# Decoder trunk on one core: another order for the opening loads, x converted chunk by chunk, 12 warm-up matmuls

## The chip, the cores and the metric

The kernel runs on one core of a Trainium2 chip. The metric is the device time of one execution in microseconds (us). The core's engines work side by side, each through its own list of instructions, and wait for each other by semaphores: TensorE (PE, matmuls), VectorE (DVE), ScalarE (ACT), GpSimd (POOL) and SyncE (SP, which here only issues DMA loads and stores). ACT and POOL can issue DMAs too.

## The reference

One layer of a decoder for 256 tokens of width 2048, in fp32. Cut to what matters here:

```python
h = rms_norm(x, ln_mix_pre)           # x * rsqrt(mean(x*x) + 1e-6) * gain
proj = h @ w_in                       # 2048 -> 6144: q, k, v of two head groups
o_sb = stick_breaking_attention(...)  # 8 heads
o_dl = dilated_mixture(...)           # 8 heads
o = rms_norm(concat(o_sb, o_dl), ln_head)
x = x + rms_norm(o @ w_out, ln_mix_post)
g, u = split(rms_norm(x, ln_ffn_pre) @ w_gate_up)
x = x + rms_norm((silu(g) * u) @ w_down, ln_ffn_post)
x = x + sigmoid(rms_norm(x, ln_pli) @ w_pli_gate) * (p @ w_pli_proj)
```

All weights are read once from HBM; that and the matmuls are most of the work. The change lies in the very first part, where h is formed and the first product h @ w_in starts.

## The kernel before

**Numbers as sums of two.** Every fp32 operand of a matmul is split into a rounded part and the remainder, `hi` and `lo`, and a product is three matmuls: hi·hi, hi·lo, lo·hi. For weights the split is line 107 (ACT, cast to `whi`) and line 108 (DVE, `wlo = wraw - whi`). For x it is done with the norm's gain at once: line 294 (ACT) makes `hT_hi = xT * g`, and line 295 (DVE) `hT_lo = xT * g - hT_hi`. The gain `g` is a column of `gT`, a tile of 128 x 64 fp32 with the scales of four norms, which is loaded once at line 197. The norm's other factor, one number a token, is applied after the product, where the banks are read out.

**The first projections.** x comes already transposed (`xT`), so that its 16 chunks of 128 features are the stationary sides of the matmuls. `gemm` walks over the 16 chunks in four groups of four (`KG`); a group's weights are three tiles, `wraw`, `whi`, `wlo`, of which the pool holds three sets (`bufs=3`). So the raw load of group 3 must wait until group 0's raw tile has been split, and so on. Each chunk takes six matmuls of 128 x 512 (two blocks of 128 tokens, three products), line 157. The first `gemm` is the projection to k of the stick-breaking heads; for it, `before=load_x` loads xT two chunks at a time (256 KB, into the memory of `y_sb`) just before the weights of these chunks are loaded (line 147). The second `gemm` (q) has `before=load_norm`: it loads x in its natural layout into the same `y_sb` (line 307), from which ACT computes the squares of the norm (line 222).

**What sets the order.** The code is written in the order of the work, but a planner sets each engine's list. Instructions inside `tc.high_priority(offset=WEIGHT_AHEAD)` rank as if they stood 200 places earlier in the code. Loads of xT and of weights, and their splits, are in such blocks; the load of gT is not. On each engine the planned list is then worked through strictly in order. A DMA that must wait, for a free buffer or for an earlier DMA that used the same semaphore, holds up all later ones of the engine that issues it.

**Warm-ups.** Before the real work PE runs ten matmuls on a zeroed tile (line 202) that feed nothing.

Of the kernel before, what the change touches and what calls it, by code (L numbers as in the profile page):

```python
# [27 lines left out]
WEIGHT_AHEAD = 200  # L28
# [6 lines left out]
def kernel(  # L35
# [38 lines left out]
    nc = tc.nc  # L74
    x, p, w_in, w_out = x[0], p[0, 0], w_in[0], w_out[0]
    w_gate_up, w_down, w_pli_gate, w_pli_proj = w_gate_up[0], w_down[0], w_pli_gate[0], w_pli_proj[0]
    out = out[0]
# [21 lines left out]
    gT = const.tile([P, 64], F32, name="gT")  # L99
# [17 lines left out]
    def tick(n=1):  # L117

        for _ in range(n):
            clock[0] += 1  # L120
            if pending and pending[0][1]():
                pending.popleft()[0]()
# [8 lines left out]
    class Chunk:  # L131
# [29 lines left out]
        def step(self, g, parts=None):  # L161

            c0, c1 = g * KG, min((g + 1) * KG, self.nk)
            halves = [(c, min(c + 2, c1)) for c in range(c0, c1, 2)]
            if parts is None:
                self.load(c0, c1)
            for a, b in halves:
                if parts is not None:
                    n = parts(a // 2)
                    for c in range(a, b, 2 // n):  # L170
                        self.load(c, c + 2 // n)
                for t in range(T):
                    self.mm(t, a, b)
                tick()
# [19 lines left out]
                evac(t, c.pm[t])  # L194


    nc.scalar.dma_start(out=gT, in_=gains)
    nc.scalar.preload_act_table_set("natural_log_exp_and_others")
    nc.vector.memset(junk, 0.0)
    warm = ps_m.tile()  # L200
    for _ in range(10):
        nc.tensor.matmul(warm, lhsT=junk[:, 0:P], rhs=junk, start=True, stop=True)
    make_identity(nc, ident)
    G_PRE, G_HEAD, G_FFN, G_PLI = 0, 16, 32, 48
# [14 lines left out]
    def token_rs(column, t):  # L219
        ss = sum_squares()  # L220
        for c in range(4):
            nc.scalar.activation(
                out=junk, in_=column(t, c), func=AF.Square,
                scale=1.0 / math.sqrt(D), accum_out=ss[:, c:c + 1])
        s1 = small.tile([P, 1], F32, name="s1")
        nc.vector.tensor_reduce(s1, ss, axis=mybir.AxisListType.X, op=ALU.add)
        return rsqrt(s1, 1)
# [41 lines left out]
    with tc.tile_pool(name="mixed", bufs=1) as mixed:  # L269
# [14 lines left out]
        xT_sb = y_sb.rearrange("q t (k m) -> q (t k) m", m=T * P)  # L284

        def load_x(g):

            with tc.high_priority(offset=WEIGHT_AHEAD):
                ks = slice(g * 2, (g + 1) * 2)
                nc.sync.dma_start(out=xT_sb[:, ks], in_=xT[:, ks])  # L290
                for kk in range(ks.start, ks.stop):
                    g_col = gT[:, G_PRE + kk:G_PRE + kk + 1]
                    h_hi = hT_hi[:, kk].rearrange("q t m -> q (t m)")
                    nc.scalar.activation(out=h_hi, in_=xT_sb[:, kk], func=AF.Copy, scale=g_col)
                    nc.vector.scalar_tensor_tensor(
                        out=hT_lo[:, kk].rearrange("q t m -> q (t m)"), in0=xT_sb[:, kk], scalar=g_col,
                        in1=h_hi.bitcast(F32), op0=ALU.mult, op1=ALU.subtract)
            return 2 if g < 2 else 1

        late = []  # L300

        def load_norm(g):

            if 1 <= g <= 4:
                sl = slice((g - 1) * NB, g * NB)
                with tc.high_priority(offset=WEIGHT_AHEAD):
                    nc.sync.dma_start(out=y_sb[:, :, sl], in_=x_v[:, :, sl])
            if g == 4:
                for t in range(T):
                    r = token_rs(lambda t, c: y_sb[:, t, c * NB:(c + 1) * NB], t)  # L310
                    rq = small.tile([P, 1], F32, name="rsq")
                    nc.vector.tensor_scalar(rq, r, 1.0 / math.sqrt(HD), None, ALU.mult)
                    rs.append(r)
                    rsq.append(rq)
                for evac, t, pm in late:
                    evac(t, pm)
            return 1


        zmask = mix.tile([P, 3, P], BF16, name="zmask")  # L320
# [1 line left out]
        for j in (0, 2):  # L322
            nc.gpsimd.affine_select(
                out=zmask[:, j, :], in_=zmask[:, j, :], pattern=[[1, P]], base=-1, channel_multiplier=-1,
# [7 lines left out]
            out=tri[:, 0:P], in_=tri[:, 0:P], pattern=[[-1, P]], base=-1, channel_multiplier=1,  # L332
# [47 lines left out]
        def parts(box, h, ts):  # L380
            x = box[0]
            if len(ts) == 2:
                return [x[:, i, h].rearrange("q t m -> q (t m)") for i in range(2)]
            return [x[:, i, h, ts[0]] for i in range(2)]
# [394 lines left out]
    def gate_out(k, np):  # L779
        s = [None, None]  # L780

        def out(t, n, x):
            with chain():
                if n == 0:
                    s[t] = temp()
                    silu(x, s[t], t)
                else:
                    gated(x, s[t], t)
                    hidden(k, np, t, s[t])
        return out  # L790
# [36 lines left out]
    parts = ((0, 4), (4, 8), (8, 11))  # L827
    for part, (j0, j1) in enumerate(parts):
        for j in range(j0, j1):
            out = gate_out(j - j0, 2 * (j1 - j0))  # L830
# [143 lines left out]
```

## Time and profile before

| | us |
|---|---|
| median of 3 runs | 1244.36 (1244.33 to 1245.23) |
| the profiled execution | 1244.12 |
| its span on the core | 1242.4 |
| gT's load issued (ACT) | 0.80 |
| first conversion of x starts (ACT) | 4.74 |
| first real matmul starts (PE) | 6.72 |

The span runs from the first instruction to the last one; 1.72 us of the execution's time lie around it. In rows of the timeline the first number is the start and the second the length, both in us, then engine, line, operation, written tile and read tiles; in square brackets stands how long the engine was idle before and what ended that. "SPq" and "ACTq" are DMA issues by these engines. In grouped rows the number behind the bar is the busy time, then the mean in ns.

### The profile page before, as it was taken

Reading aid. Unit: us, or ns where it says so; the run is one execution under the profiler, and the core shown is the slowest. Engines: PE = TensorE matmul, PEld = TensorE weight load, DVE = VectorE, ACT = ScalarE, POOL = GpSimd, SP = SyncE. Lnnn points to the kernel's source line nnn. Section 1 sums busy time; section 2 is a strip of 40 time slices with the busy share of each in tenths; the row PEclk is TensorE's granted clock in tenths of the full one; section 3 lists DMA queues with packets and bytes.
Section 4 is the critical chain, followed back from the end, with each engine's and each line's share of the span. In section 5 each row is a group of like instructions: output and inputs, shape, how many; then the busy total and the mean of one; then the engine's idle time right before and its main releaser. Section 6 shows DMA issues by size and latency. Waiting matters only on the chain.

```text
span 1242.4 us, 14323 instructions
## 1 busy us (share of the span) xinstructions
PE 1231.7 (99%) x5503; PEld 992.7 (80%) x5503; DVE 941.9 (76%) x975; ACT 652.3 (53%) x738; POOL 31.1 (3%) x57
## 2 busy tenths in 40 slices
PE   9999999999999999999999999999999999999997
PEld 6887888888888888888888888888777888887886
DVE  6575564545554868988888798889878888888887
ACT  6654554454443746555544555555453555655553
POOL 0001000000100200000000000000000000001000
PEclk9999999999999999999999999999999999999999
DMA  9744744455655845556555555655555565657761
GB/s 343 266 148 169 254 149 161 165 169 170 245 195 178 282 150 181 192 204 214 178 190 198 198 177 200 236 168 197 180 180 192 203 212 173 246 175 241 241 202 69
DMA packets 123172, 245.10 MB, mean 197 GB/s; under 512 B 6960, under 2 KB 7264, under 8 KB 122720
## 3 DMA queue, kind: packets, MB, share of 16 engines
q1 hardware_dynamic: 120320, 233.07, 55.2%
q0 software_dynamic: 2528, 11.02, 2.4%
q8 instruction: 43, 0.70, 0.2%
q14 instruction: 25, 0.20, 0.1%
q10 hardware_dynamic: 256, 0.10, 0.0%
HBM read 238.91 MB, written 6.83 MB: 198 GB/s over the span
## 4 chain that ended last, share of the span: by engine, by line
PE 93%; DVE 3%; ACT 1%; issue 1%; DMA 1%; POOL 0%; DVEq 0%; SPq 0%; ACTq 0%; POOLq 0%
PE bank L675 62%; PE bank L157 27%; DVE wlo L108 1%; ACT whi L107 1%; PE bank L686 1%; PE bank L378 1%; PE bank L233 1%; PE bank L348 1%; DMA wraw<-in_w_pli_gate_dram 0%; DMA gT<-in_gains_dram 0%; DVE temp L898 0%; PE bank L391 0%; PE bank L390 0%; PE bank L389 0%; PE bank L416 0%
## 5 line engine op out<-in xcount | busy, mean ns | idle before, releaser
L108 DVE TENSOR_TENSOR wlo<-wraw,whi 128x2048 fp32r<-128x2048 f32 (+3 forms) x229 | 465.2, 2040 | 198.3 <-ACT whi L107 197.7
L107 ACT CAST whi<-wraw 128x2048 fp32r<-128x2048 f32 (+3 forms) x229 | 390.5, 1709 | 371.0 <-PE bank L675 207.8
L675 PE MATMUL bank<-whi,hT_hi 128*128 128x512 f32 x667 | 262.5, 397 | 0.2 <-ACT whi L107 0.2
L675 PE MATMUL bank<-wlo,hT_hi 128*128 128x512 f32 x667 | 261.9, 395 | 0.5 <-DVE wlo L108 0.4
L675 PE MATMUL bank<-whi,hT_lo 128*128 128x512 f32 x667 | 261.6, 395 | 0.0
L157 PE MATMUL bank<-whi,hT_hi 128*128 128x512 f32 x384 | 157.2, 410 | 1.0 <-ACT whi L107 1.0
L157 PE MATMUL bank<-whi,hT_lo 128*128 128x512 f32 x384 | 152.3, 397 | 0.0
L157 PE MATMUL bank<-wlo,hT_hi 128*128 128x512 f32 x384 | 152.2, 396 | 0.0
L675 PEld LDWEIGHTS bank<-wlo,hT_hi 128*128 128x128 f32 x667 | 125.2, 188 | 31.7 <-DVE wlo L108 1.5
L675 PEld LDWEIGHTS bank<-whi,hT_hi 128*128 128x128 f32 x667 | 125.1, 188 | 30.6 <-ACT whi L107 0.9
L675 PEld LDWEIGHTS bank<-whi,hT_lo 128*128 128x128 f32 x667 | 125.2, 188 | 29.9
L649 DVE TENSOR_TENSOR wlo<-wsum,whi 128x2048 fp32r<-128x2048 f32 x47 | 107.6, 2288 | 12.9 <-ACT whi L648 12.8
L675 PE MATMUL bank<-wlo,fT_hi 128*128 128x512 f32 x282 | 111.2, 396 | 0.5 <-DVE wlo L108 0.5
L675 PE MATMUL bank<-whi,fT_hi 128*128 128x512 f32 x282 | 110.9, 397 | 0.2 <-ACT whi L107 0.2
L675 PE MATMUL bank<-whi,fT_lo 128*128 128x512 f32 x282 | 110.9, 396 | 0.0
L157 PEld LDWEIGHTS bank<-whi,hT_lo 128*128 128x128 f32 x384 | 72.5, 189 | 17.7
L157 PEld LDWEIGHTS bank<-whi,hT_hi 128*128 128x128 f32 x384 | 72.6, 189 | 16.8 <-ACT whi L107 1.9
L157 PEld LDWEIGHTS bank<-wlo,hT_hi 128*128 128x128 f32 x384 | 72.8, 189 | 14.5 <-DVE wlo L108 0.3
L641 DVE TENSOR_TENSOR wsum<-wraw 128x1024 f32<-128x1024 f32 x47 | 57.4, 1221 | 11.3 <-DMA wraw<-in_w_down_dram 5.9
L647 ACT CAST whi<-wsum 128x1024 fp32r<-128x1024 f32 x47 | 49.5, 1052 | 29.1 <-PE bank L675 27.8
L675 PEld LDWEIGHTS bank<-wlo,fT_hi 128*128 128x128 f32 x282 | 53.0, 188 | 14.1 <-DVE wlo L108 1.5
L675 PEld LDWEIGHTS bank<-whi,fT_hi 128*128 128x128 f32 x282 | 52.9, 188 | 13.4 <-ACT whi L107 0.9
(174 smaller groups left out, 1421.0 us busy)
## 6 DMA issues: line engine op xcount, KB each, us to landing
wraw<-in_w_gate_up_dram SPq DMA_DIRECT2D x176, 512.0 KB, 4.8
wraw<-in_w_down_dram SPq DMA_DIRECT2D x88, 512.0 KB, 5.2
wraw<-in_w_in_dram SPq DMA_DIRECT2D x40, 1024.0 KB, 5.2
wraw<-in_w_out_dram SPq DMA_DIRECT2D x16, 1024.0 KB, 5.0
wraw<-in_w_pli_gate_dram SPq DMA_DIRECT2D x32, 512.0 KB, 5.2
wraw<-in_w_in_dram SPq DMA_DIRECT2D x14, 512.0 KB, 8.3
y_sb<-in_xT_dram SPq DMA_DIRECT2D x8, 256.0 KB, 7.2
y_sb<-in_x_dram SPq DMA_DIRECT2D x4, 512.0 KB, 9.4
```

The costliest lines, as they stand in the source:

```text
L107: nc.scalar.copy(hi, raw)
L108: nc.vector.tensor_tensor(lo, raw, hi.bitcast(F32), ALU.subtract)
L157: nc.tensor.matmul(self.pm[t], lhsT=a[:, c, t, :], rhs=b[:, c % KG, :], start=c == 0 and a is a_hi and b is hi, stop=c == self.nk - 1 and ...
L233: nc.tensor.transpose(out=pt[:, k * P:(k + 1) * P], in_=x_sb[c][:, t, k * P:(k + 1) * P], identity=ident)
L348: nc.tensor.transpose(out=pt[:, h * P:(h + 1) * P], in_=nat[:, h * P:(h + 1) * P], identity=ident)
L378: nc.tensor.matmul(out, lhsT=a[u], rhs=b[w], start=i == 0, stop=i == 2)
L641: nc.vector.tensor_tensor(s[:, 0:2], raw[:, 0:1].to_broadcast([P, 2, NB]), raw[:, 1:4:2], ALU.add)
L647: nc.scalar.copy(shi[:, 0:2], s[:, 0:2])
L649: nc.vector.tensor_tensor(slo, s, shi.bitcast(F32), ALU.subtract)
L675: nc.tensor.matmul(pm, lhsT=a[u], rhs=w[v], start=first and x == 0 and y == 0, stop=last and x == len(terms) - 1 and y == 2)
L686: nc.tensor.transpose(out=pt[:, c * P:(c + 1) * P], in_=f[:, c * P:(c + 1) * P], identity=ident)
```

## The change

Three edits in the opening. The load of gT moves from ACT's instruction stream to SP's. The first piece of xT (chunks 0 and 1) is issued by ACT, the other seven by SP as before. The conversion of x leaves `load_x` for a function `convert_x`, which `step` calls for as many chunks as the next weight load covers: one at a time in the first two pairs of chunks, two at a time later. And there are 12 warm-up matmuls, not 10.

```diff
@@ Chunk.step
             for a, b in halves:
                 if parts is not None:
-                    n = parts(a // 2)
+                    n, convert = parts(a // 2)
                     for c in range(a, b, 2 // n):
+                        convert(c, c + 2 // n)
                         self.load(c, c + 2 // n)
@@ start of the program
-    nc.scalar.dma_start(out=gT, in_=gains)
+    nc.sync.dma_start(out=gT, in_=gains)
     nc.scalar.preload_act_table_set("natural_log_exp_and_others")
     nc.vector.memset(junk, 0.0)
     warm = ps_m.tile()
-    for _ in range(10):
+    for _ in range(12):
         nc.tensor.matmul(warm, lhsT=junk[:, 0:P], rhs=junk, start=True, stop=True)
@@ load_x
             with tc.high_priority(offset=WEIGHT_AHEAD):
                 ks = slice(g * 2, (g + 1) * 2)
-                nc.sync.dma_start(out=xT_sb[:, ks], in_=xT[:, ks])
-                for kk in range(ks.start, ks.stop):
+                (nc.sync if g else nc.scalar).dma_start(out=xT_sb[:, ks], in_=xT[:, ks])
+            return 2 if g < 2 else 1, convert_x
+
+        def convert_x(c0, c1):
+            with tc.high_priority(offset=WEIGHT_AHEAD):
+                for kk in range(c0, c1):
                     g_col = gT[:, G_PRE + kk:G_PRE + kk + 1]
                     h_hi = hT_hi[:, kk].rearrange("q t m -> q (t m)")
                     nc.scalar.activation(out=h_hi, in_=xT_sb[:, kk], func=AF.Copy, scale=g_col)
                     nc.vector.scalar_tensor_tensor(
                         out=hT_lo[:, kk].rearrange("q t m -> q (t m)"), in0=xT_sb[:, kk], scalar=g_col,
                         in1=h_hi.bitcast(F32), op0=ALU.mult, op1=ALU.subtract)
-            return 2 if g < 2 else 1
@@ load_norm
-            return 1
+            return 1, lambda c0, c1: None
```

The planned lists of three engines change in the opening. First SP's loads, from its first on (`y_sb<-in_xT_dram` is a piece of xT, `wraw` weights, a trailing x4 means four such rows). Before:

```order
L290 DMA y_sb<-in_xT_dram 128x512
L147 DMA wraw<-in_w_in_dram 128x512 x4
L290 DMA y_sb<-in_xT_dram 128x512 x2
L147 DMA wraw<-in_w_in_dram 128x2x512
L290 DMA y_sb<-in_xT_dram 128x512
L147 DMA wraw<-in_w_in_dram 128x2x512
```

In the change, the same list from the eleventh to the twenty-second load, with what each waits for (DMAHW is an earlier DMA's semaphore, DVE_49 a buffer that DVE has to free):

```order
L147 DMA wraw<-in_w_in_dram 128x2x512 [waits DMAHW3_49]
L291 DMA y_sb<-in_xT_dram 128x512 [waits DMAHW4_49]
L147 DMA wraw<-in_w_in_dram 128x2x512 [waits DMAHW5_49]
L291 DMA y_sb<-in_xT_dram 128x512 [waits DMAHW6_49]
L147 DMA wraw<-in_w_in_dram 128x2x512 [waits DMAHW7_49,DVE_49]
L291 DMA y_sb<-in_xT_dram 128x512 [waits DMAHW0_49]
L147 DMA wraw<-in_w_in_dram 128x2x512 [waits DMAHW1_49]
L147 DMA wraw<-in_w_in_dram 128x2x512 [waits DMAHW2_49,DVE_49]
L147 DMA wraw<-in_w_in_dram 128x2x512 [waits DMAHW3_49]
L147 DMA wraw<-in_w_in_dram 128x2x512 [waits DMAHW5_49,DMAHW4_49,DVE_49]
L147 DMA wraw<-in_w_in_dram 128x2x512
L198 DMA gT<-in_gains_dram 128x64 [waits DMAHW6_49]
```

The load of gT (line 198 of the new code) stands behind seven pieces of xT and fourteen weight loads, three of which wait for DVE; before it was ACT's first instruction. Behind it on SP come the four loads of x for the norm, the load of pT and the weights of the third group of the second projection. Second, ACT's list at the start of the program. Before:

```order
L197 DMA gT<-in_gains_dram 128x64
L198 ACT_TABLE_LOAD
L294 ACTIVATE hT_hi<-y_sb,gT 128x256 x2
L107 CAST whi<-wraw 128x512 x4
L294 ACTIVATE hT_hi<-y_sb,gT 128x256 x4
L107 CAST whi<-wraw 128x1024
L294 ACTIVATE hT_hi<-y_sb,gT 128x256 x2
```

In the change:

```order
L291 DMA y_sb<-in_xT_dram 128x512
L199 ACT_TABLE_LOAD
L107 CAST whi<-wraw 128x512 x4
L107 CAST whi<-wraw 128x1024 x4
L299 ACTIVATE hT_hi<-y_sb,gT 128x256 x16
L107 CAST whi<-wraw 128x1024 x2
L223 ACTIVATE junk,ss<-y_sb 128x512 x4
L107 CAST whi<-wraw 128x1024 x2
```

All sixteen conversions of x now stand in one block behind the casts of the first three groups of weights; the squares of the norm (line 223) and the casts follow. Third, DVE's list has moved the same way: before, its first work on x and on weights was

```order
L295 SCALAR_TENSOR_TENSOR hT_lo<-y_sb,gT,hT_hi 128x256 x2
L108 TENSOR_TENSOR wlo<-wraw,whi 128x512 x4
L295 SCALAR_TENSOR_TENSOR hT_lo<-y_sb,gT,hT_hi 128x256 x2
L334 CAST ntri<-tmp 128x128
L295 SCALAR_TENSOR_TENSOR hT_lo<-y_sb,gT,hT_hi 128x256 x2
```

and in the change it is

```order
L108 TENSOR_TENSOR wlo<-wraw,whi 128x512 x4
L338 CAST ntri<-tmp 128x128
L108 TENSOR_TENSOR wlo<-wraw,whi 128x1024 x4
L300 SCALAR_TENSOR_TENSOR hT_lo<-y_sb,gT,hT_hi 128x256 x16
L108 TENSOR_TENSOR wlo<-wraw,whi 128x1024 x2
```

DVE's splits of the first three groups stand ahead of all sixteen of x, and those that free the raw buffers for SP don't depend on gT. PE's list has the two more warm-ups and some swaps among the first matmuls, and is otherwise the same.

## The prediction

> **What bounds the kernel now.** I read the page first, for the share of each engine and the chain of waits.
>
> ```profile
> span 1242.4 us, 14323 instructions
> PE 1231.7 (99%) x5503; PEld 992.7 (80%) x5503; DVE 941.9 (76%) x975; ACT 652.3 (53%) x738; POOL 31.1 (3%) x57
> PE 93%; DVE 3%; ACT 1%; issue 1%; DMA 1%; POOL 0%; DVEq 0%; SPq 0%; ACTq 0%; POOLq 0%
> ```
>
> TensorE (PE) is busy in 99% of the span and carries 93% of the chain that ends last. Next I looked at what PE ever waits for, and at the stretch after its first real matmul.
>
> ```profile
> PE bank L202 <- DVE junk L199: 1.3, 1, 1.3
> PE bank L157 <- ACT whi L107: 1.0, 1, 1.0
> PE bank L675 <- DVE wlo L108: 0.9, 2, 0.5
> ...
> 6.72:1242.40 1235.68, 1227.30 (x5493) 991.37 (x5493) 939.53 (x965) 649.03 (x733) 29.54 (x47) 1.00 0.58 197
> ```
>
> The two longest waits of PE lie in the opening. After 6.72 us it is idle for 1235.68 - 1227.30 = 8.4 us, and part of that is the tail behind the last matmul. So a later first matmul moves the end by nearly the same amount: at most 8.4 us could be taken up. The one question is when the first L157 matmul starts. The timeline of the opening answers it for the kernel before:
>
> ```profile
> 0.80 0.41 ACTq L197 DMA_DIRECT2D gT<-in_gains_dram  x1
> 0.81 0.38 SPq L290 DMA_DIRECT2D y_sb<-in_xT_dram  x1
> 1.24 1.84 SPq L147 DMA_DIRECT2D wraw<-in_w_in_dram  x4
> 1.26 4.45 PE L202 MATMUL bank<-junk 128*128 128x512 bf16 x10 [1.26 <-DVE junk L199]
> 3.13 0.91 SPq L290 DMA_DIRECT2D y_sb<-in_xT_dram  x2
> 4.74 0.91 ACT L294 ACTIVATE hT_hi<-y_sb,gT 128x256 fp32r<-128x256 f32 x2 [2.20 <-DMA gT<-in_gains_dram]
> 5.28 0.88 DVE L295 SCALAR_TENSOR_TENSOR hT_lo<-y_sb,gT,hT_hi 128x256 fp32r<-128x256 f32 x2 [3.41 <-ACT hT_hi L294]
> 5.55 1.64 ACT L107 CAST whi<-wraw 128x512 fp32r<-128x512 f32 x3
> 6.72 1.22 PE L157 MATMUL bank<-whi,hT_hi 128*128 128x512 f32 x2 [1.02 <-ACT whi L107]
> ```
>
> ScalarE (ACT) waits for gT, the norm scales. They are asked for at 0.80 and usable at 4.74; conversion of x and of the weights follows, and PE starts at 6.72.
>
> **The change, part by part.** *The place of the gT load.* The line is now issued by sync (SP), but the planned order has it behind twenty-one others: seven of the eight pieces of xT (the first is on ScalarE's queue) and fourteen weight loads. Everything that makes hT waits for gT, and every real matmul reads hT. So I need gT's landing.
>
> Bytes ahead of it: xT, 8 pieces of 256 KB, is 2.10 MB; the weights are six groups of 1 MB, four of the first projection and two of the second (4 x 256 KB and 10 x 512 KB), 6.29 MB; together 8.39 MB. The sizes and their times to land stand in the DMA view of 0 to 60 us:
>
> ```profile
> wraw<-in_w_in_dram SPq DMA_DIRECT2D x14, 512.0 KB, 8.3
> y_sb<-in_xT_dram SPq DMA_DIRECT2D x8, 256.0 KB, 7.2
> wraw<-in_w_in_dram SPq DMA_DIRECT2D x4, 256.0 KB, 4.2
> gT<-in_gains_dram ACTq DMA_DIRECT2D x1, 32.0 KB, 3.9
> ```
>
> A 512 KB load takes 8.3 us here though the queue moves that much in 1.4 us at the rates below: loads of this queue wait behind those issued earlier. How fast they drain is in the windows (last two columns: DMA share and GB/s):
>
> ```profile
> 0.00:10.00 10.00, 7.72 (x18) 3.79 (x19) 5.00 (x16) 5.52 (x10) 1.53 (x10) 1.00 0.78 246
> 10.00:14.00 4.00, 4.00 (x19) 3.21 (x18) 3.25 (x8) 3.53 (x7) 0.00 (x0) 1.00 1.05 400
> 14.00:20.00 6.00, 6.00 (x28) 4.79 (x27) 5.79 (x8) 5.31 (x9) 0.00 (x0) 1.00 1.05 387
> 20.00:26.00 6.00, 6.00 (x27) 4.81 (x26) 4.60 (x7) 4.78 (x8) 0.00 (x0) 1.00 1.05 387
> ```
>
> The DMA share is full from 10 us on, so the rate cannot rise with another order. Moved by 10, 14, 20 and 26 us: 2.46, 4.06, 6.38 and 8.70 MB. The gap between "moved" and "usable" comes from three casts that waited for their weights:
>
> ```profile
> 12.88 1.05 ACT L107 CAST whi<-wraw 128x1024 fp32r<-128x1024 f32 x1 [0.19 <-DMA wraw<-in_w_in_dram]
> ...
> 14.90 1.05 ACT L107 CAST whi<-wraw 128x1024 fp32r<-128x1024 f32 x1 [0.16 <-DMA wraw<-in_w_in_dram]
> ...
> 16.93 1.05 ACT L107 CAST whi<-wraw 128x1024 fp32r<-128x1024 f32 x1 [0.16 <-DMA wraw<-in_w_in_dram]
> ```
>
> By the order of issue, 3.15, 3.93 and 4.72 MB had been asked for up to these loads; they are moved at 11.7, 13.7 and 15.7 us, and the casts start 1.2 us later each time.
>
> When does SP issue gT? The two weight loads just ahead need the third raw buffer back, which VectorE (DVE) frees when it has split the last half of group 2. In the new order that load too stands behind 4.72 MB, so it is usable at about 16.9, then cast and split:
>
> ```profile
> L108 DVE TENSOR_TENSOR wlo<-wraw,whi 128x1024 fp32r<-128x1024 f32 x14 | 17.2, 1225 | 7.8 <-ACT whi L107 7.6
> L107 ACT CAST whi<-wraw 128x1024 fp32r<-128x1024 f32 x14 | 14.7, 1047 | 4.6 <-DMA wraw<-in_w_in_dram 4.6
> L294 ACT ACTIVATE hT_hi<-y_sb,gT 128x256 fp32r<-128x256 f32 x16 | 7.0, 498 | 2.6 <-DMA gT<-in_gains_dram 2.2 <-DMA y_sb<-in_xT_dram 0.4
> L295 DVE SCALAR_TENSOR_TENSOR hT_lo<-y_sb,gT,hT_hi 128x256 fp32r<-128x256 f32 x16 | 6.9, 479 | 3.7 <-ACT hT_hi L294 3.7
> ...
> 19.27 0.88 SPq L147 DMA_DIRECT2D wraw<-in_w_in_dram  x2
> ```
>
> 16.9 + 1.05 + 1.23 with small steps between is 19.3; two issues of 0.44 us each bring gT's own issue to 20.2. By then 6.46 MB have moved, so 1.93 MB are still ahead: 5.0 us, to 25.2. gT's 32 KB take 0.1 us, and 1.2 us of landing make **26.5**. ScalarE then makes the first piece of hT in the 0.54 us that lie between its 4.74 and DVE's 5.28 above, and PE starts at **27.05**, 20.3 us later than 6.72. All weights of three groups are split by then, and three more groups lie raw in the buffers.
>
> *Behind the start.* ACT and DVE convert one chunk of x in about 0.45 us each (498 and 479 ns, starts overlapping), and PE uses six matmuls on it, 1.4 us at the spacing of the row below: no second wait there. Behind gT on SP stand the four loads of x for the norm, pT, and the weights of group 6. The x loads need parts of y_sb that DVE frees 4.4 to 7.1 us after the start; the last lands by about +11; the squares, at 0.75 us each, let pT go at +10 and group 6 at +11.5, landing near +15. PE reaches group 6 after 144 matmuls, 33.6 us. The cover is 18 us, less about 10 for the casts that wait for their buffers and for nat, so 8 us: I cost it at nothing.
>
> *Chunk by chunk conversion, x's first load on ScalarE's queue, two more warm-ups.* With gT at 26.5 none of these is on the path: the first x has landed 20 us earlier, and twelve warm-ups end at 1.26 + 12 x 0.43 = 6.4 us, inside PE's wait. Their cover is that wait; without it two warm-ups would cost 0.85 us. pT's earlier split only uses DVE's time beside PE.
>
> *The slow first matmuls.* The matmul row of the opening against the steady pace:
>
> ```profile
> 8.17 0.63 PE L157 MATMUL bank<-whi,hT_lo 128*128 128x512 f32 x1
> 8.60 0.63 PE L157 MATMUL bank<-whi,hT_hi 128*128 128x512 f32 x1
> ...
> 9.88 0.43 PE L157 MATMUL bank<-wlo,hT_hi 128*128 128x512 f32 x1
> 10.15 0.39 PE L157 MATMUL bank<-whi,hT_lo 128*128 128x512 f32 x1
> ...
> 107.80 11.20 PE bank L157 x48
> ```
>
> Matmuls start every 0.43 us up to 9.88 and every 0.233 us (11.20 / 48) later, while the clock column stays at 1.00. Eight real matmuls are slow, at 8 x 0.195 = 1.6 us. Now PE rests for some 20 us, which no row before shows. Bounds: no slow matmul at all, -1.6; or as many as in the whole opening, 10 + 8, +1.9. The nearest row is the start from rest at 1.26, where all ten warm-ups (4.45 us) stayed slow, so at least two more than eight; I take +0.5.
>
> The Trainium skill, "TensorE: Matmul & The Clock Gate", Part 1, says that an idle window of some 3.4 us halves PE's clock and that one busy window of the same length, running freely, restores it. By that rule the restart costs an estimated 1.5 to 3.1 us against the 1.6 of now, so the end would be 20.3 to 21.8 us later; the spacing at 1.26 and 9.88 agrees with it, and a long gap is not in this trace.
>
> *Sum.* The profiled execution took 1244.12 us, 1.72 more than its span and 0.24 less than the median. 1244.1 + 20.3 + 0.5 = **1264.9 us**.
>
> **Rivals.** *The small load overtakes.* If gT's packets don't wait for the 1.93 MB, it lands the 3.9 us of its row after its issue: 20.2 + 3.9 = 24.1, PE starts at 24.65, and the time is 1262.5. For it: 32 KB is small. Against: the 8.3 us of the 512 KB loads. The Trainium skill's "DMA: Bandwidth & Descriptors", Queues, rings and completion order, has each engine consume one queue's descriptors in ring order, against this rival; the row on 512 KB agrees.
>
> *The loads behind gT come too late.* SP sits in the wait for DVE with the queue empty, and ScalarE's squares hold back pT and with it group 6. If the 8 us of cover is missed by 4, the time is 1269. For it: ACT's order now has four squares ahead of the casts of the second projection. Against: the slack above, and the raw weights already loaded.
>
> *gT does come first, as the few words say.* Then it is usable at 4.7 as now, only one chunk is converted ahead of its weights, and the twelve warm-ups set the start: 6.6 instead of 6.72, with no gap in which the clock falls back, at best 1.6 us less. That gives 1242.5 to 1244: not slower. It decides if SP sends gT ahead of the weights. Against: SP's rows before (one piece of xT, four of weights, two of xT) are its planned list in order.
>
> *It is absorbed.* PE's idle 8.4 us would leave +12: 1256. Against: those gaps wait for DVE and for weights at places that shift with the start.
>
> **How the numbers follow.** The forecast has 0.80, overtaking 0.06, late loads 0.06, gT first 0.04, absorbed 0.02, and 0.02 is for what I don't see (half of it faster). The forecast's own bounds: the early drain could be as fast as the later one (400 GB/s from 4 us on: 1.0 us earlier), landing up to 1 us later, slow matmuls -1.6 to +1.9; one us off each way in issue. Taken together 1262.3 to 1267.3; with overtaking and a part of the late loads the range is 1261.6 to 1267.8. About 0.2%, 2.5 us, is what a measurement can tell from no change. Even "gT first" ends within 0.2% of the 1244.4 shown, so it makes up no change: 0.04; faster 0.01 and slower 0.95, where "absorbed", "late loads" and "overtaking" all fall.
>
> **What would show it.** In the profile after: ACT's first hT_hi (L299) near 26.5 with gT named as what ended some 8.5 us of idle; SP's gT (L198) issued near 20; PE's first L157 near 27 with an idle time of about 20 us; gaps below 1 us afterwards; DMA nearly still from 27 to 31 us. It is wrong if gT is issued among SP's first loads, if PE starts before 23 us, or if PE has a second wait of over 2 us before 70 us.

## The result, and the profile after

| | before | after |
|---|---|---|
| median | 1244.67 us (1244.33 to 1245.23, 4 runs) | 1264.43 us (1263.87 to 1264.55, 4 runs) |
| the profiled execution | 1244.12 us | 1264.35 us |
| its span | 1242.4 us | 1262.6 us |

The ratio of after to before is 1.0161, with a 95% interval of 1.0146 to 1.0176: the change makes the kernel slower by 1.6%, near 20 us.

The page of the kernel after, its span, its engines and the shares of the chain of waits:

```profile
span 1262.6 us, 14327 instructions
PE 1232.9 (98%) x5505; PEld 993.8 (79%) x5505; DVE 942.0 (75%) x975; ACT 652.2 (52%) x738; POOL 31.0 (2%) x57
PE 92%; DVE 3%; DMA 2%; ACT 1%; issue 1%; SPq 0%; POOL 0%; DVEq 0%; ACTq 0%; POOLq 0%
```

PE's busy time has grown by 1.2 us and the span by 20.2. So PE does nothing for some 19 us more than before. What it waits for stands in its waits (total, times, longest, in us), the first rows:

```profile
PE bank L157 <- ACT hT_hi L299: 19.8, 1, 19.8
PE bank L679 <- DVE wlo L108: 1.3, 3, 0.5
PE bank L203 <- DVE junk L200: 1.3, 1, 1.3
```

One wait of 19.8 us, for the first piece of hT; the next is 1.3 us in three parts. The timeline of the opening shows how that wait is made:

```profile
0.80 0.42 ACTq L291 DMA_DIRECT2D y_sb<-in_xT_dram  x1
0.81 1.33 SPq L147 DMA_DIRECT2D wraw<-in_w_in_dram  x3
1.26 5.30 PE L203 MATMUL bank<-junk 128*128 128x512 bf16 x12 [1.26 <-DVE junk L200]
...
12.10 7.30 SPq L147 DMA_DIRECT2D wraw<-in_w_in_dram  x5
...
16.18 1.04 ACT L107 CAST whi<-wraw 128x1024 fp32r<-128x1024 f32 x1 [1.00 <-DMA wraw<-in_w_in_dram]
17.26 1.23 DVE L108 TENSOR_TENSOR wlo<-wraw,whi 128x1024 fp32r<-128x1024 f32 x1 [0.82 <-ACT whi L107]
19.44 0.47 SPq L198 DMA_DIRECT2D gT<-in_gains_dram  x1
25.78 6.50 ACT L299 ACTIVATE hT_hi<-y_sb,gT 128x256 fp32r<-128x256 f32 x16 [8.56 <-DMA gT<-in_gains_dram]
26.34 0.80 PE L157 MATMUL bank<-whi,hT_hi 128*128 128x512 f32 x1 [19.78 <-ACT hT_hi L299]
...
30.35 0.50 PE L157 MATMUL bank<-whi,hT_hi 128*128 128x512 f32 x1
30.69 0.39 PE L157 MATMUL bank<-wlo,hT_hi 128*128 128x512 f32 x1
```

SP issues gT at 19.44, when DVE's split of 17.26 to 18.49 has freed the buffer that the weight loads ahead of it waited for. ACT, idle for 8.56 us, is released by gT at 25.78, and PE starts at 26.34. The windows say what the loads did meanwhile, and what follows behind PE's start (the last three columns are the granted clock, the DMA share and GB/s):

```profile
0.00:19.44 19.44, 5.30 (x12) 1.64 (x12) 8.72 (x17) 7.93 (x9) 1.51 (x10) 0.76 0.91 324
19.44:25.00 5.56, 0.00 (x0) 0.00 (x0) 0.00 (x0) 0.00 (x0) 0.00 (x0) 0.50 1.04 380
25.00:26.00 1.00, 0.00 (x0) 0.00 (x0) 0.00 (x0) 0.22 (x1) 0.00 (x0) 0.50 0.07 15
26.00:28.00 2.00, 1.66 (x4) 1.37 (x5) 1.68 (x5) 2.00 (x6) 0.00 (x0) 0.50 0.00 0
...
26.34:1262.60 1236.26, 1227.62 (x5493) 992.15 (x5493) 933.25 (x958) 643.71 (x728) 29.49 (x47) 1.00 0.57 191
```

By 19.44 us 19.44 x 324 = 6.30 MB have moved; 2.09 of the 8.39 MB are still ahead of gT, and 5.56 x 380 = 2.11 MB move before the DMA falls still at 25.0. No engine computes anything in these 5.56 us: they all wait for 32 KB. From PE's first real matmul to the end it is 1236.26 us now, 1235.68 before.

This accounts for all of it: the start is 26.34 - 6.72 = 19.62 later, PE's busy time behind it is 1227.62 - 1227.30 = 0.32 longer, and its idle time there 8.64 - 8.38 = 0.26. The sum is 20.2, as the spans differ.

### The profile page after: what moved, and what is told of

It reads as the page before. It is cut to its first block, busy times and chain, and to the rows that moved or that the text cites. A ratio compares the mean times of both kernels' runs of the same rounds, so it can differ in the third digit from the quotient of the medians.

```text
span 1262.6 us, 14327 instructions
## 1 busy us (share of the span) xinstructions
PE 1232.9 (98%) x5505; PEld 993.8 (79%) x5505; DVE 942.0 (75%) x975; ACT 652.2 (52%) x738; POOL 31.0 (2%) x57
## 4 chain that ended last, share of the span: by engine, by line
PE 92%; DVE 3%; DMA 2%; ACT 1%; issue 1%; SPq 0%; POOL 0%; DVEq 0%; ACTq 0%; POOLq 0%
PE bank L679 61%; PE bank L157 27%; DVE wlo L108 1%; ACT whi L107 1%; PE bank L690 1%; PE bank L382 1%; DMA wraw<-in_w_in_dram 1%; PE bank L234 1%; PE bank L352 1%; DMA gT<-in_gains_dram 1%; DMA wraw<-in_w_gate_up_dram 0%; DMA y_sb<-in_xT_dram 0%; PE bank L394 0%; PE bank L395 0%; PE bank L393 0%
## 5 line engine op out<-in xcount | busy, mean ns | idle before, releaser
L157 PE MATMUL bank<-whi,hT_hi 128*128 128x512 f32 x384 | 157.7, 411 | 19.8 <-ACT hT_hi L299 19.8
```

Source lines behind the costliest of these rows:

```text
L157: nc.tensor.matmul(self.pm[t], lhsT=a[:, c, t, :], rhs=b[:, c % KG, :], start=c == 0 and a is a_hi and b is hi, stop=c == self.nk - 1 and ...
```

## The experiments

Two theories were to be told apart. Mine: the place of gT's load on SP's list makes the whole loss, through PE's start. The rival: other parts of the change (x on ACT's queue, conversion chunk by chunk, the warm-ups) cost or save something too, or the load would be late for another reason. All diffs are against the changed kernel unless it is said otherwise. "Before" is the kernel before, timed on the same chip with them.

### The load ahead of all others on the same queue

```diff
-    nc.sync.dma_start(out=gT, in_=gains)
+    with tc.high_priority(offset=CHAIN_AHEAD):
+        nc.sync.dma_start(out=gT, in_=gains)
```

> The changed kernel with one edit: gT's load on SP gets a rank 1000 places earlier, so that it is SP's first load, as the few words on the change say. Theory (gT's place on SP's list is the whole loss): gT usable near 4.7 us, PE's first real matmul at 6.2 to 6.8 us without a gap behind the warm-ups, time 1243.0 to 1244.6, at or a little below the kernel before. Rival (the blockwise conversion or x on ScalarE's queue costs it too): PE starts after 10 us and the time stays above 1250.

1243.50 us (11 runs); before 1244.10 (21 runs); ratio 0.9999, 0.9990 to 1.0008. Timeline of this kernel:

```profile
0.81 0.39 SPq L199 DMA_DIRECT2D gT<-in_gains_dram  x1
...
4.41 0.91 ACT L300 ACTIVATE hT_hi<-y_sb,gT 128x256 fp32r<-128x256 f32 x2 [1.87 <-DMA y_sb<-in_xT_dram]
...
6.41 0.88 PE L157 MATMUL bank<-whi,hT_hi 128*128 128x512 f32 x2
...
7.54 0.39 PE L157 MATMUL bank<-whi,hT_lo 128*128 128x512 f32 x1
```

With gT as SP's first load, the whole loss is gone and all other parts of the change are still there. Now ACT waits for x, not for gT, and PE starts 0.3 us earlier than before. That is too little to see in the time: with gT's load in front, the change makes no difference within 0.1%.

### The load on ACT's queue again

```diff
-    nc.sync.dma_start(out=gT, in_=gains)
+    nc.scalar.dma_start(out=gT, in_=gains)
```

> The changed kernel with gT's load given back to ScalarE's queue, where it stands second, behind x's first 256 KB. Theory: the 20 us are gone; gT usable near 5 us, PE's first real matmul at 6.2 to 7.0 us, 1243.0 to 1245.0. Rival (conversion chunk by chunk is what costs): above 1250.

1243.43 us (11 runs); ratio 0.9996, 0.9988 to 1.0005. gT is now ACT's second load, behind the first piece of x, issued at 1.25. It released ACT at 6.13, 1.1 us later than I had written, so that ACT cast the first weights meanwhile; PE still starts at 6.69. The end is as expected, the way to it was not. Neither the queue nor the place within ACT's first two loads matters at this size.

### The load moved, alone

Against the kernel before:

```diff
-    nc.scalar.dma_start(out=gT, in_=gains)
+    nc.sync.dma_start(out=gT, in_=gains)
```

> The kernel before with one edit: gT's load on SP, without a rank, ten warm-ups, conversion by pairs. Theory: gT stands behind 8 pieces of xT and 14 weight loads (8.4 MB) and is usable at 25.5 to 26.5, PE's first real matmul at 26 to 27, 1264 to 1265.2: this part alone is the whole change. Rival (the loss needs the other parts): below 1255.

1266.78 us (1264.71 to 1268.18, 4 runs); ratio 1.0183, 1.0169 to 1.0197. Its timeline and waits:

```profile
20.06 0.47 SPq L197 DMA_DIRECT2D gT<-in_gains_dram  x1
27.07 6.51 ACT L294 ACTIVATE hT_hi<-y_sb,gT 128x256 fp32r<-128x256 f32 x16 [9.22 <-DMA gT<-in_gains_dram]
27.63 0.79 PE L157 MATMUL bank<-whi,hT_hi 128*128 128x512 f32 x1 [21.92 <-ACT hT_hi L294]
...
PE bank L675 <- DVE wlo L108: 2.4, 5, 1.0
```

This one line makes the loss by itself, and 1.6 us more than I had put as the upper end. The profiled execution is the longest of the four, 1268.18 us. Three parts are seen in it against the profile of the change: PE starts 1.3 us later than in the change, its slow matmuls last to 33 us and not to 30.5 (below), and the waits for `wlo` later on are 2.4 us and not 1.3.

### The load moved, and the first piece of x on ACT

Against the kernel before:

```diff
-    nc.scalar.dma_start(out=gT, in_=gains)
+    nc.sync.dma_start(out=gT, in_=gains)
...
-                nc.sync.dma_start(out=xT_sb[:, ks], in_=xT[:, ks])
+                (nc.sync if g else nc.scalar).dma_start(out=xT_sb[:, ks], in_=xT[:, ks])
```

> The kernel before with two of the edits, gT's load on SP and x's first piece on ScalarE's queue; conversion by pairs, ten warm-ups. All planned lists are then those of the changed kernel but for the two warm-ups. Theory: 1263.8 to 1265.0, as the changed kernel; with the 1266.8 of gT's load alone this makes the move of x's first piece a gain of some 2 us in this position. Rival (the 2.4 us between the changed kernel and gT's load alone come from the warm-ups): 1266 to 1267.5.

1265.16 us (1264.47 to 1266.36, 4 runs); ratio 1.0172, 1.0159 to 1.0186. On the opening's lists this is the changed kernel but for two warm-ups. It lies just above what I had written, and at the 1265.32 us that the changed kernel itself took when it was run again (below). So with gT late, the chunk-by-chunk conversion and the warm-ups are worth nothing that can be seen; the intervals leave room for some 2.5 us either way. Whether x on ACT's queue gives back the 1.6 us that lie between this run and the one before it stays open: the four runs of each overlap.

### The warm-ups alone

Against the kernel before:

```diff
-    for _ in range(10):
+    for _ in range(12):
```

> The kernel before with twelve warm-ups instead of ten, nothing else. Theory: they end at 6.6 us, just before the first real matmul at 6.7, so PE does not rest, is slow for two to eight real matmuls fewer, and the time falls by 0.3 to 1.6 us against the kernel before (at most 0.13%: hardly to be told by time, but by the spacing of the first matmuls). Rival (they delay the real work): the first real matmul starts later than 6.8 us and the time grows.

1243.46 us (11 runs); before 1243.72 (15 runs); ratio 0.9998, 0.9989 to 1.0007: no time can be told from it. In the profiled execution the warm-ups took 4.61 us and ended at 5.87, not at 6.6 as I had written; PE's real matmuls start at 6.46 and run at full pace from 7.6 us on, and not from 10. How much of that comes from the two more warm-ups isn't shown: the same twelve took 5.30 us in the profile of the change and 4.24 in that of its repeat, so the point at which PE comes to full pace differs from one execution to the next.

### The load half way up

```diff
-    nc.sync.dma_start(out=gT, in_=gains)
+    with tc.high_priority(offset=100):
+        nc.sync.dma_start(out=gT, in_=gains)
```

> The changed kernel with gT's rank raised by 100 places: on SP it now stands behind 4.7 MB, not 8.4. Theory: the start moves with gT and the end with the start, one to one: gT usable before 17.3, the conversions follow the cast of the third group at about 17.2 to 18, PE's first real matmul at 17.7 to 18.6, and the time lies above the kernel before by that start less 6.7, plus or minus 1: 1255 to 1257. Rival (loads that come too late behind gT add to the loss, or slack absorbs a part): the time is off by more than 2 us from that line.

1256.65 us (one run). Its timeline:

```profile
9.10 0.33 SPq L199 DMA_DIRECT2D gT<-in_gains_dram  x1
...
16.59 1.04 ACT L107 CAST whi<-wraw 128x1024 fp32r<-128x1024 f32 x1 [1.01 <-DMA wraw<-in_w_in_dram]
17.54 6.49 ACT L300 ACTIVATE hT_hi<-y_sb,gT 128x256 fp32r<-128x256 f32 x16
...
18.10 0.79 PE L157 MATMUL bank<-whi,hT_hi 128*128 128x512 f32 x1 [12.70 <-ACT hT_hi L300]
```

This is the dose: with gT in the middle of the list PE starts at 18.10 and the execution takes 1256.65. What ACT waits for last is not gT here, which landed 7.6 us after its issue, at 16.7, but the weights of the third group: their cast stands ahead of all conversions on ACT's list. From there to the changed kernel's profiled one it is 8.24 us of start and 7.70 of time; from the kernel before, 11.38 of start and 12.53 of time, with 1.25 us more of PE's busy time behind the start (1228.55 against 1227.30). The end follows the start nearly one to one, at two points.

### The load from another queue at a late time

To see whether gT waits for its own queue or for all that is in flight, ACT issues it late. GpSimd writes zeros into gT's tile a number of times first, which the load has to wait for; the tile is made twice as wide to slow these writes.

```diff
-    gT = const.tile([P, 64], F32, name="gT")
+    gT = const.tile([P, 128], F32, name="gT")
...
-    nc.sync.dma_start(out=gT, in_=gains)
...
+        for _ in range(52):    # 80 in the first of the two
+            nc.gpsimd.memset(gT, 0.0)
+        nc.scalar.dma_start(out=gT[:, 0:64], in_=gains)
```

With 80:

> The changed kernel, but gT's load is issued by ScalarE, and only behind its casts of the first three groups (GpSimd's zeroing of the gT tile, 80 times, holds it until then): near 17.3 us, while some 3 MB of weights and x stand in SP's queue; SP's list has no gT in it. Theory (behind its issue gT waited for the loads ahead of it in SP's own queue): it lands 2.5 to 4 us after its issue, at 20 to 21.5, PE's first real matmul at 20.5 to 22, time 1258 to 1260. Rival (a load waits for all the bytes under way, whichever queue they are in): it lands at 25 or later, PE starts at 25.5 or later, 1263 to 1265.

1265.28 us (2 runs). Each write took 0.26 us, so ACT issued the load at 22.93 only, when SP's loads were nearly done; it landed at 26.13. That tells nothing apart.

With 52:

> The changed kernel with gT's load issued by ScalarE behind its casts of the first three groups, as with 80 zeroings, whose 0.26 us each held the load until 22.9 us; now there are 52, done by about 16 us, so that ScalarE's last cast lets it go at 17.3 to 17.7 us, with some 3 MB still ahead in SP's queue. Theory (in SP's queue gT waited for the loads ahead of it): it lands 2.5 to 4 us after its issue, at 20 to 21.7, PE's first real matmul at 20.5 to 22.3, 1258 to 1260. Rival (a load waits for all bytes under way in both queues): it lands at 25 or later, and the time is 1263 to 1265.

1260.29 us (1259.91 to 1260.67, 2 runs); ratio 1.0131, 1.0110 to 1.0151. Timeline and windows:

```profile
16.93 0.34 ACTq L340 DMA_DIRECT2D gT<-in_gains_dram  x1
...
19.19 0.88 SPq L147 DMA_DIRECT2D wraw<-in_w_in_dram  x2
...
22.23 6.49 ACT L298 ACTIVATE hT_hi<-y_sb,gT 128x256 fp32r<-128x256 f32 x16 [4.33 <-DMA gT<-in_gains_dram]
22.79 0.80 PE L157 MATMUL bank<-whi,hT_hi 128*128 128x512 f32 x1 [17.22 <-ACT hT_hi L298]
...
0.00:16.93 16.93, 4.31 (x12) 1.49 (x12) 7.49 (x16) 6.96 (x9) 12.09 (x62) 0.73 0.89 321
16.93:22.23 5.30, 0.00 (x0) 0.00 (x0) 1.23 (x1) 0.97 (x1) 0.00 (x0) 0.50 1.06 382
```

At 16.93 us 5.43 MB have moved, so 2.96 of the 8.39 MB are to come. But the last two weight loads, 1.05 MB, are issued by SP only at 19.19, behind gT; under way at gT's issue were 1.91 MB. The "25 or later" of the rival had counted all 2.96. Had gT waited for the 1.91, they would have moved by 21.9 (at 382 GB/s), and with the 0.8 us from there to use that the change shows (25.0 to 25.78), gT would have come at 22.7. ACT could use it at 22.23, between the two theories. The packets of the two queues (packets, MB, share; q1 is SP's queue, q10 ACT's) say more. From 17.0 to 20.6 us, then from 20.6 to 21.6 us:

```profile
q1 hardware_dynamic: 734, 1.39, 105.5%
...
q1 hardware_dynamic: 169, 0.33, 92.3%
q10 hardware_dynamic: 144, 0.03, 16.0%
```

ACT's queue moves nothing up to 20.6, while SP's moves 1.39 MB; then gT goes between SP's packets. So it passed some 0.5 MB at its first packet, and 0.2 MB at its last (21.5 us), of the 1.91 that were under way at its issue. At 382 GB/s that is a gain of 0.5 to 1.3 us. So the run doesn't bear out my theory that only the loads of its own queue hold gT up: 5.3 us went by from issue to use, with the DMA engines full, against 3.9 in the still opening of the kernel before, and I had written 2.5 to 4. By this run, another queue would have gained the change little once so much was under way.

### PE kept busy until gT lands

Here the changed kernel gets more warm-ups, so that PE's rest becomes short or goes away; the line that loads gT moves behind them in the code, so that its place on SP's list stays what it was. What the extra matmuls compute isn't used.

```diff
-    nc.sync.dma_start(out=gT, in_=gains)
-    nc.scalar.preload_act_table_set("natural_log_exp_and_others")
     nc.vector.memset(junk, 0.0)
     warm = ps_m.tile()
+    for _ in range(83):    # 96 in the second
+        nc.tensor.matmul(warm, lhsT=junk[:, 0:P], rhs=junk, start=True, stop=True)
+    nc.sync.dma_start(out=gT, in_=gains)
+    nc.scalar.preload_act_table_set("natural_log_exp_and_others")
     for _ in range(12):
```

With 95 in all:

> The changed kernel with 95 warm-up matmuls instead of 12, gT at the same place of SP's list. They fill PE's wait up to about 25 us (some 16 at 0.43 us, the others at 0.22). Theory (after 20 us of rest the first ten real matmuls run at 0.43 us instead of 0.233): all real matmuls start 0.233 us apart from the first on, and the time falls by 1.9 us to 1262.0 to 1263.0. Rival (the slow spacing belongs to the first matmuls on fresh operands, not to the rest): the first real ones still stand 0.43 us apart, and the time stays at 1264 to 1265.

1265.38 us (1264.37 to 1266.31, 4 runs); ratio 1.0173, 1.0159 to 1.0187. I had expected 1262 to 1263. The warm-ups ended at 23.4, and gT came at 26.74:

```profile
27.30 0.50 PE L157 MATMUL bank<-whi,hT_hi 128*128 128x512 f32 x1 [3.90 <-ACT hT_hi L301]
27.64 0.40 PE L157 MATMUL bank<-wlo,hT_hi 128*128 128x512 f32 x1
27.87 0.49 PE L157 MATMUL bank<-whi,hT_lo 128*128 128x512 f32 x1
28.16 0.62 PE L157 MATMUL bank<-whi,hT_hi 128*128 128x512 f32 x1
...
31.57 0.40 PE L157 MATMUL bank<-whi,hT_lo 128*128 128x512 f32 x1
```

A rest of 3.9 us was left, and after three fast matmuls PE fell back to a spacing of 0.43 us from 28.16 to 31.57.

With 108 in all, beside the changed kernel once more on the same chip:

> The changed kernel with 108 warm-up matmuls: by the spacing seen with 95 of them (the last ends at 23.4 us) they end at about 26.2, so that PE rests for 0.3 to 1.5 us, not 3.9. Theory (rest slows PE a few us later, and for 3.4 us): no real matmul stands 0.43 us apart, and the time is 1.5 to 2 us below the changed kernel on the same chip, 0.5 us of that lost if gT lands before the fill ends. Rival (the slow spacing does not come from the rest): nine to fourteen slow ones again, no difference in time.

> The changed kernel itself once more, beside the run with 108 warm-ups on the same chip. Theory: gT usable at 25.8 to 26.8, PE's first real matmul 0.55 us later, nine to fourteen slow matmuls, 1263.8 to 1265.5.

1263.15 us (1262.77 to 1264.15, 4 runs) against 1265.32 (1264.63 to 1266.01, 4 runs) for the change; ratios to before 1.0155 (1.0140 to 1.0170) and 1.0171 (1.0154 to 1.0188). The kernel with 108 warm-ups:

```profile
27.54 0.50 PE L157 MATMUL bank<-whi,hT_hi 128*128 128x512 f32 x1 [1.01 <-ACT hT_hi L301]
27.87 0.39 PE L157 MATMUL bank<-wlo,hT_hi 128*128 128x512 f32 x1
...
27.54:1261.10 1233.56, 1225.26 (x5493) 990.84 (x5493) 933.36 (x958) 643.77 (x728) 29.50 (x47) 1.00 0.57 192
```

No matmul is slow, and PE's busy time behind the start is 1225.26 us, 2.4 below the changed kernel's 1227.62. It gains 2.2 us over the change although its PE starts 0.5 us later than in the repeat (27.54 against 27.03). So the rest does cost about 2.4 us at its end. But the kernel before pays 1227.30 - 1225.26 = 2.0 us of it already, for its own opening; the change adds 0.3.

No version here beats the kernel before by an amount that its interval doesn't reach: the best three stand within 0.1% of it.

## Why the prediction was right, step by step

Forecast 1264.9 us, in a range of 1261.6 to 1267.8; measured 1264.43. The forecast's mechanism is what the trace shows.

**gT's issue: 20.2 predicted, 19.44 found.** The step that carries it is the last split of group 2, predicted to end at 19.3 and ended at 18.49. Its weights were usable 0.7 us earlier than I had worked out (cast at 16.18, not 16.9). The two issues of SP behind that split took the 0.9 us that I had put for them.

**Landing: 26.5 predicted, 25.78 found.** The bytes ahead were right: 2.09 MB at issue (1.93 predicted), drained at 380 GB/s by 25.0. From there to use it was 0.8 us, where I had taken 1.2 from three casts; 0.4 us of the 0.7 lie here.

**PE's start: 27.05 predicted, 26.34 found,** so +19.6 and not +20.3. The 0.56 us of ACT between the two are as in the row that I used. In the repeat of the same kernel the three steps were 20.15, 26.47 and 27.03: the miss of 0.7 us is within what changes from one execution to the next.

**Slow matmuls: +0.5 predicted, +0.3 found** in this execution, by PE's busy time. The quantity isn't a constant, though (last section): busy time behind the start was 0.5 above the kernel before in the repeat, and 1.5 in the run with the move alone. The Trainium skill, "TensorE: Matmul & The Clock Gate", Part 1, says of the clock that it is set by windows of some 3.4 us that run freely; the clock's falls and rises in the last section agree with it: they lie whole multiples of 3.41 us apart, at another phase in each execution. By that rule I had given 20.3 to 21.8 us for start and restart together, and found 20.2.

**Nothing behind the start: right.** PE's idle time behind it was 8.64 us against 8.38, its longest wait there 0.5 us. The x for the norm, pT and group 6, all behind gT on SP, were covered.

**The other three edits at nothing: right** as far as the runs can tell. With gT early, the first two runs and the warm-ups alone show it to 0.1%. With gT late, the run with x on ACT agrees with the change, and that the move alone took 1.6 us more than that run stays open.

**The rivals.** *The small load overtakes* is refuted in its own queue (6.3 us from issue to landing, 2.1 MB drained first). In another queue it passed 0.2 to 0.5 of 1.9 MB, which the rival didn't speak of. *The loads behind gT come too late* would have shown a second wait; there is none over 0.5 us. *gT comes first* is not what SP did, but the run that makes it so gave 1243.5 us, within the 1242.5 to 1244 of that rival's price. *Absorbed*: the start moved the end by its full amount, at 18.10 and at 26.34.

**Where expectations of the runs missed.** The move alone came out 1.6 us above its range: its PE started 1.3 us later than the change's and was busy for 1.2 us longer behind that (1228.78 against 1227.62). The 95 warm-ups came out 2.4 above theirs: PE started at 27.30, 1.0 later than in the change, and the rest that was left cost 1.8 us of PE's time (1227.09 against the 1225.26 without one). That a load on ACT's queue takes 2.5 to 4 us under full traffic was an estimate from still moments of the DMA; it took 5.3, for it waited for most of what SP had under way.

## What to carry to other kernels

Where a planner ranks loads, a load without a rank can sink behind ranked ones of its engine whose lines stand further down in the code; here it sank behind 21 of them. So read the planned list of the queue, not the line: ask of a small load what stands ahead of it in its own queue, add up these bytes, divide by the rate of the windows, and ask which engine's first instruction needs it. If that engine is the one that is busy in 98% of the span, each microsecond comes out at the end.

## What the runs showed of the hardware that I had not expected

PE's granted clock changes on a grid of 3.41 us. In the windows of 0.2 us in which the clock column changes, its value says at which point the change came. The kernel after:

```profile
10.00:10.20 0.20, 0.00 (x0) 0.00 (x0) 0.00 (x0) 0.10 (x1) 0.00 (x0) 0.75 0.97 379
30.40:30.60 0.20, 0.20 (x2) 0.20 (x1) 0.20 (x2) 0.20 (x2) 0.00 (x0) 0.55 0.00 0
```

0.75 is half of the window at 1.00 and half at 0.50, so the clock fell at 10.10; 0.55 is a tenth at 1.00, so it rose at 30.58. The kernel with 95 warm-ups, in the same way:

```profile
28.00:28.20 0.20, 0.20 (x3) 0.15 (x3) 0.20 (x2) 0.20 (x2) 0.00 (x0) 0.88 0.00 0
31.40:31.60 0.20, 0.20 (x2) 0.11 (x2) 0.20 (x1) 0.20 (x2) 0.00 (x0) 0.59 0.00 0
```

And so for the others, each from two such windows:

| kernel | PE's first real matmul | clock fell | clock rose | between | slow from the start for | PE busy behind the start |
|---|---|---|---|---|---|---|
| after | 26.34 | 10.10 | 30.58 | 20.48 = 6 x 3.413 | 4.24 us | 1227.62 |
| the change again | 27.03 | 7.69 | 31.58 | 23.89 = 7 x 3.413 | 4.55 | 1227.76 |
| the move alone | 27.63 | 9.39 | 33.29 | 23.90 = 7 x 3.414 | 5.66 | 1228.78 |
| move and x on ACT | 26.98 | 9.17 | 33.06 | 23.89 = 7 x 3.413 | 6.08 | 1229.02 |
| half way up | 18.10 | 7.50 | 24.57 | 17.07 = 5 x 3.414 | 6.47 | 1228.55 |
| 95 warm-ups | 27.30 | 28.15 | 31.56 | 3.41 | 3.41 (from 28.15) | 1227.09 |
| 108 warm-ups | 27.54 | not | | | 0 | 1225.26 |

The grid's phase differs from execution to execution: the changed kernel saw its clock fall at 10.10 in one and at 7.69 in another. So the slow stretch behind the start, 3.4 to 6.5 us here, is partly chance. Against the kernel with 108 warm-ups, PE was busy for 1.8 to 3.8 us longer behind these starts. The spacing (0.43 us instead of 0.233, so 46% of the slow stretch) gives 1.6 to 3.0 of that; up to 1.0 us is left open. That the phase makes part of the scatter between runs of such a kernel is likely, but wasn't tested. A rest of 3.9 us was enough to lose the clock, and one of 1.0 was not. Nor does a stretch of the grid that PE fills for the most part always bring it back: half way up, PE was busy for 3.04 of the 3.42 us from 17.74 to 21.16, and the clock rose only at the end of the next stretch, at 24.57.

Two more. In the opening of the kernels before and after, the clock column says 1.00 while the warm-ups start 0.43 us apart, so before its first change it can't be read. And GpSimd's writes of 128 x 128 zeros followed each other every 0.26 us.
